# Linear attention on one core: loads and stores for 16 heads at once, with K and V on interleaved partitions

## The chip, the cores and the metric

One core of one Trainium2 chip. The metric is the device time of one execution in microseconds (us); lower is better. The profiled span is some 1.7 us shorter than that time. A run is called slow when it is over 1.5% above the fastest of the same kernel; only fast runs are compared.

## The reference

For 8 x 12 = 96 heads of 512 rows and 64 columns:

```python
Q_feat = np.maximum(0, Q) + 1
K_feat = np.maximum(0, K) + 1
KV = np.einsum('bhkd,bhkv->bhdv', K_feat, V)
K_sum = np.sum(K_feat, axis=2)
numerator = np.einsum('bhqd,bhdv->bhqv', Q_feat, KV)
denominator = np.einsum('bhqd,bhd->bhq', Q_feat, K_sum)
return (numerator / (denominator[:, :, :, None] + 1e-10)).astype(np.float32)
```

All tensors are fp32: 37.75 MB are read and 12.58 MB written.

## The kernel before

It works in 12 groups of 8 heads. A group loads K, V and Q (1 MB each, cast to bf16 on the way), makes features of K and Q on VectorE, multiplies K by V on TensorE (`keys_values`), transposes Q on TensorE with ScalarE copying the result out (`transposes`), and multiplies and normalises (`output`). Loads run three groups ahead, stores three behind. V lies in a block-diagonal tile of mostly zeros, so that four heads share a matmul.

```python
def load_v(g):
    for b in range(4):                       # four heads, 32 partitions each
        nc.gpsimd.dma_start(
            out=v_blk[g % NV][32 * b : 32 * b + 32, b],
            in_=v_dram[32 * b : 32 * b + 32, 2 * g : 2 * g + 2])

def keys_values(g):                          # 128 rows by 64 columns
    ...
    for c in range(C2):
        for n in range(2):
            nc.tensor.matmul(kva_ps[64 * n : 64 * n + 64],
                lhsT=kf[:, c, n, :], rhs=vb[:, :, n, c, :],
                start=(c == 0), stop=(c == C2 - 1))
    ...                                      # ScalarE copies it out

for g in range(NG - 1):
    if g:
        k_features(g)
        q_features(g)
        transposes(g - 1)
    if g >= 2:
        output(g - 2)
    keys_values(g)
    if g + AHEAD < NG:
        load_k(g + AHEAD); load_v(g + AHEAD); load_q(g + AHEAD)
    if g >= LAG:
        store(g - LAG)
last = NG - 1
k_features(last)
transposes(last - 1)
output(last - 2)
q_features(last)
keys_values(last)
transposes(last)
output(last - 1)
output(last)
for g in range(last - LAG, NG):
    store(g)                                 # the last two on SyncE, in halves
```

In these traces VectorE takes its instructions in program order: one that waits for data (8.36 us for Q at one place below) holds up everything behind it.

## Time and profile before

| | kernel before |
|---|---|
| time, median of the first runs | 127.61 us (127.33 to 127.71) |
| profiled span | 126.0 us |
| DMA rate over the span | 400 GB/s of HBM traffic |
| busiest compute engine | TensorE, 55% |

Here is what the end looks like: busy time of each engine in stretches of 4 us (from the start of the span; x is the number of instructions), then the granted TensorE clock, the mean busy share of the 16 DMA engines, and GB/s.

```profile
112.00:116.00 4.00, 2.46 (x40) 1.68 (x40) 3.83 (x11) 1.34 (x2) 0.00 (x0) 0.75 1.03 418
116.00:120.00 4.00, 0.95 (x14) 0.47 (x10) 2.05 (x5) 0.00 (x0) 0.00 (x0) 0.50 1.02 411
120.00:124.00 4.00, 0.00 (x0) 0.00 (x0) 0.00 (x0) 0.00 (x0) 0.00 (x0) 0.50 0.95 366
```

The columns of busy time are TensorE, its weight loads, VectorE, ScalarE and GpSimd. Computing ends in the second stretch (VectorE is busy for 2.05 us of it, then no more), while the DMA engines stay full for another 6 us. Stores are queued up, and computing hides beneath them. A DMA share over 1 means that packets of one engine overlap a little.

### The profile page before, as it was taken

How to read it: one execution, taken by the hardware profiler on the slowest of the kernel's cores; microseconds unless marked ns; L12 is line 12 of the kernel's file. 1: busy time of each engine (PE TensorE's matmuls, PEld its weight loads, DVE VectorE, ACT ScalarE, POOL GpSimd, SP SyncE). 2: the span in 40 equal slices, each digit the busy share in tenths (PEclk: the TensorE clock that was granted, in tenths of full speed). 3: DMA queues.
4: the chain of work that ended last, by engine and by line, in shares of the span. 5: the costliest groups of instructions: out<-in, count | busy, mean ns of one | idle time of the engine just before them, and what ended most of it. 6: DMA issues, size and time to landing. Idle time of an engine off the chain costs nothing.

```text
span 126.0 us, 2374 instructions
## 1 busy us (share of the span) xinstructions
PE 69.4 (55%) x960; PEld 51.1 (41%) x960; DVE 66.3 (53%) x155; ACT 47.1 (37%) x76; POOL 53.4 (42%) x91
## 2 busy tenths in 40 slices
PE   0000099719859089682971980890693496966100
PEld 0000087507647067462750660670562365744100
DVE  4898802077193582938607605723921944769400
ACT  7950007930645505554073054036019009290000
POOL 6695785616346156452372274263353341200000
PEclk9999999995999976999599589679869959996555
DMA  3999999999999999999999999999999999999993
GB/s 82 337 208 213 204 208 208 212 212 208 211 206 213 207 208 213 206 298 293 200 252 336 198 213 370 213 209 360 228 208 321 267 206 284 425 410 418 413 403 121
DMA packets 14186, 32.13 MB, mean 255 GB/s; under 512 B 1376, under 2 KB 1376, under 8 KB 14176
## 3 DMA queue, kind: packets, MB, share of 16 engines
q0 software_dynamic: 12816, 28.84, 98.8%
q1 hardware_dynamic: 1360, 3.15, 6.7%
q8 instruction: 7, 0.11, 0.3%
q14 instruction: 3, 0.02, 0.0%
HBM read 37.75 MB, written 12.58 MB: 400 GB/s over the span
## 4 chain that ended last, share of the span: by engine, by line
DMA 67%; DVE 9%; PE 8%; POOL 6%; issue 4%; POOLq 0%
DMA k_raw<-in_K_dram 25%; DMA q_raw<-in_Q_dram 17%; DMA v_blk<-in_V_dram 16%; DMA out_dram<-o_sb 9%; DVE o_sb L184 7%; PE kva_ps L141 5%; POOL v_blk L93 4%; POOL q_raw L100 2%; PE qt_ps L160 2%; DVE recip L183 1%; PE o_ps L173 1%; DVE qf L116 1%; POOL k_raw L86 1%; POOL zero L195 0%; POOLq L100 0%
## 5 line engine op out<-in xcount | busy, mean ns | idle before, releaser
L141 PE MATMUL kva_ps<-v_blk,kf 128*64 128x320 bf16 x384 | 40.6, 385 | 15.8 <-DMA v_blk<-in_V_dram 15.8
L141 PEld LDWEIGHTS <-kf 128*64 128x64 bf16 x384 | 27.9, 143 | 24.8 <-DVE qf L116 15.8
L93 POOL DMA_DIRECT2D v_blk<-in_V_dram x48 | 26.3, 552 | 27.0 <-DMA k_raw<-in_K_dram 14.8
L173 PE MATMUL o_ps<-kva_diag,qt 128*64 128x130 bf16 x384 | 19.1, 234 | 32.0 <-DVE o_sb L184 31.3
L184 DVE TENSOR_TENSOR o_sb<-o_ps,recip 128x512 f32<-128x512 f32 x48 | 33.2, 691 | 1.6
L151 ACT CAST kva_diag<-kva_ps 64x256 bf16<-64x256 f32 x24 | 8.9, 372 | 65.2 <-PE kva_ps L141 64.9
L161 ACT COPY qt<-qt_ps 128x1024 bf16<-128x1024 bf16 x24 | 29.5, 1301 | 0.3
L173 PEld LDWEIGHTS <-qt 128*64 128x64 bf16 x384 | 12.7, 114 | 37.5 <-DVE o_sb L184 35.8
L116 DVE TENSOR_SCALAR qf<-q_raw 128x1024 bf16<-128x1024 bf16 x24 | 9.2, 424 | 32.9 <-DMA q_raw<-in_Q_dram 32.9
L116 DVE TENSOR_SCALAR kf<-k_raw 128x1024 bf16<-128x1024 bf16 (+1 forms) x24 | 10.9, 497 | 10.3 <-DMA k_raw<-in_K_dram 10.3
L107 POOL DMA_DIRECT2D out_dram<-o_sb x10 | 7.7, 774 | 16.1 <-DMA q_raw<-in_Q_dram 7.8
L160 PE MATMUL qt_ps<-identity,qf 128*128 128x128 bf16 x192 | 13.1, 223 | 0.0
L160 PEld LDWEIGHTS <-qf 128*128 128x128 bf16 x192 | 11.1, 99 | 3.4 <-issue 3.2
L183 DVE RECIPROCAL recip<-o_ps 128x8 f32<-128x8 f32 x48 | 9.5, 198 | 4.1 <-PE o_ps L173 4.1
L86 POOL DMA_DIRECT2D k_raw<-in_K_dram x11 | 7.8, 713 | 8.4 <-DMA out_dram<-o_sb 3.7
L100 POOL DMA_DIRECT2D q_raw<-in_Q_dram x12 | 8.8, 730 | 4.4 <-DMA v_blk<-in_V_dram 2.5
L152 ACT CAST kva_diag<-kva_ps 64x4 bf16<-64x4 f32 x24 | 4.0, 168 | 0.0
L206 DVE MEMSET v_blk<- 128x2925 f32 x1 | 2.5, 2496 | 0.7 <-DVE ones L202 0.7
L224 DVE MEMSET v_blk<- 128x2925 f32 x1 | 2.5, 2496 | 0.6 <-issue 0.6
L212 DVE MEMSET v_blk<- 128x2925 f32 x1 | 2.5, 2496 | 0.6 <-issue 0.6
L219 POOL MEMSET kva_diag<- 128x520 bf16 x3 | 2.0, 720 | 0.0
L207 ACT COPY v_blk<-zero 128x2195 f32<-128x2195 f32 x1 | 2.0, 2020 | 0.0
(15 smaller groups left out, 7.9 us busy)
## 6 DMA issues: line engine op xcount, KB each, us to landing
out_dram<-o_sb POOLq DMA_DIRECT2D x10, 1024.0 KB, 12.1
q_raw<-in_Q_dram POOLq DMA_DIRECT2D x12, 512.0 KB, 11.1
v_blk<-in_V_dram POOLq DMA_DIRECT2D x48, 128.0 KB, 9.5
k_raw<-in_K_dram POOLq DMA_DIRECT2D x11, 512.0 KB, 12.0
out_dram<-o_sb SPq DMA_DIRECT2D x4, 512.0 KB, 7.6
k_raw<-in_K_dram SPq DMA_DIRECT2D x1, 1024.0 KB, 5.0
```

The lines of the kernel that those rows point to most:

```text
L86: (nc.sync if g == 0 else nc.gpsimd).dma_start(out=k_raw, in_=k_dram[:, g * 2 : g * 2 + 2])
L93: nc.gpsimd.dma_start(out=v_blk[g % NV][32 * b : 32 * b + 32, b], in_=v_dram[32 * b : 32 * b + 32, 2 * g : 2 * g + 2],)
L100: nc.gpsimd.dma_start(out=q_raw, in_=q_dram[:, g * 2 : g * 2 + 2])
L107: nc.gpsimd.dma_start(out=o_to, in_=o_sb)
L116: nc.vector.tensor_scalar(out=dst, in0=src, scalar1=1.0, scalar2=1.0, op0=ALU.add, op1=ALU.max)
L141: nc.tensor.matmul(kva_ps[64 * n : 64 * n + 64], lhsT=kf[:, c, n, :], rhs=vb[:, :, n, c, :], start=(c == 0), stop=(c == C2 - 1),)
L151: nc.scalar.copy(out=kva[ps, :, n, 0:D], in_=kva_ps[ps, 0:4, :])
L160: nc.tensor.transpose(qt_ps[:, c, :], qf[:, half * C + c, :, :], identity)
L161: nc.scalar.copy(out=qt[:, :, :, half], in_=qt_ps)
L173: nc.tensor.matmul(ops[c // 4][64 * j : 64 * j + 64, c // 2 % 2, (c % 2) * W : (c % 2) * W + W], lhsT=qt[:, c, 32 * b : 32 * b + 32, :], r ...
L183: nc.vector.reciprocal(out=recip, in_=cells[:, :, :, :, D:D1])
L184: nc.vector.tensor_tensor(out=o_sb[:, h:NP:2, 4 * i : 4 * i + 4].rearrange("p n (b c) d -> p b c n d", b=2), in0=cells[:, :, :, :, 0:D], i ...
```

## The change

The intent is fewer and larger transfers. The unit of loads and stores becomes a stage of 16 heads (2 MB a tensor, six stages), each still computed as two groups. K and V come in two DMAs, each to every second partition, so that a partition half holds one head of each of two pairs. V's block tile then needs two blocks instead of four, and the first matmul becomes two row tiles of 64 rows by 128 columns. The loop and its end are rewritten for stages. The diff, cut to its core:

```diff
-    def load_v(g):
-        for b in range(4):
+    def load_v(s):
+        for e in range(2):
             nc.gpsimd.dma_start(
-                out=v_blk[g % NV][32 * b : 32 * b + 32, b],
-                in_=v_dram[32 * b : 32 * b + 32, 2 * g : 2 * g + 2],
+                out=v_blk[s % IN_BUFS][e:P:2, M * e : M * e + M],
+                in_=v_dram[e, :, M * s : M * s + M],
             )
...
         for c in range(C2):
-            for n in range(2):
+            for r in range(2):
+                ps = slice(64 * r, 64 * r + 64)
                 nc.tensor.matmul(
-                    kva_ps[64 * n : 64 * n + 64],
-                    lhsT=kf[:, c, n, :],
-                    rhs=vb[:, :, n, c, :],
+                    kva_ps[:, r, 0 : NB * D],
+                    lhsT=kf[ps, c, :, :],
+                    rhs=vb[ps, :, c, :],
...
+        for g in range(2, NG - 2):
+            k_features(g)
+            q_features(g)
+            if g > 2:
                 transposes(g - 1)
+            output(g - 2) if g > 2 else None
+            keys_values(g)
+            if g % 2:
+                s = g // 2
+                store(s - 1)
+                if s + 2 < NS:
+                    load_k(s + 2)
+                    load_v(s + 2)
+                    load_q(s + 2, parts=2 if s + 2 == NS - 1 else 1)
+        a, b = NG - 2, NG - 1
+        k_features(a)
+        k_features(b)
+        transposes(a - 1)
+        output(a - 2)
+        keys_values(a)
+        output(a - 1)
+        keys_values(b)
+        store(NS - 2)
+        q_features(a)
+        transposes(a)
+        q_features(b)
+        transposes(b)
+        output(a)
+        output(b)
+        store(NS - 1)                        # four pieces on SyncE
```

More of the change, by code (lines that the diff above doesn't have):

```diff
@@ L13 @@
 BANK = 512
-IN_BUFS = 4
-OUT_BUFS = 6
-LAG = 3
-AHEAD = 3
+IN_BUFS = 3
+OUT_BUFS = 3
 @with_exitstack
@@ L42 @@
     C2 = 2 * C
-    NPAIR = B * H * S // (P * C)
-    NP = 4
-    NG = NPAIR // NP
+    M = 4
+    NS = B * H // (4 * M)
+    NG = 2 * NS
     D1 = D + 1
     W = 2 * D1
-    def view(t, c):
-        return t.flatten_outer_dims().rearrange("(n p c) d -> p n c d", p=P, c=c)
-    q_dram = view(Q, C2)
-    k_dram = view(K, C2)
-    v_dram = view(V, C2)
-    o_dram = view(out, C)
+    NB = 5
+    q_dram = Q.flatten_outer_dims().rearrange("(m p c) d -> p m c d", p=P, c=C2)
+    k_dram, v_dram = (
+        t.flatten_outer_dims().rearrange("(m e q c) d -> e q m c d", e=2, q=64, c=C2)
+        for t in (K, V)
+    )
+    o_dram = out.flatten_outer_dims().rearrange("(n p c) d -> p n c d", p=P, c=C)
     const = ctx.enter_context(tc.tile_pool(name="const", bufs=1))
@@ L63 @@
     recip_pool = ctx.enter_context(tc.tile_pool(name="recip", bufs=4))
-    psum_kva = ctx.enter_context(tc.tile_pool(name="psum_kva", bufs=2, space=bass.MemoryType.PSUM))
+    psum_kva = ctx.enter_context(tc.tile_pool(name="psum_kva", bufs=1, space=bass.MemoryType.PSUM))
     psum = ctx.enter_context(tc.tile_pool(name="psum", bufs=2, space=bass.MemoryType.PSUM))
@@ L68 @@
     identity = const.tile([P, P], BF16, name="identity")
-    NV = 3
-    v_blk = [const.tile([P, 5, 2, C2, D], BF16, name=f"v_blk{i}") for i in range(NV)]
-    ones = const.tile([P, 4], BF16, name="ones")
+    v_blk = [const.tile([P, 2 * NB, C2, D], BF16, name=f"v_blk{i}") for i in range(IN_BUFS)]
+    ones = const.tile([P, 2], BF16, name="ones")
     zero = const.tile([P, 1], FP32, name="zero")
-    kva_diag = [const.tile([P, 4, 2, D1], BF16, name=f"kva_diag{i}") for i in range(NV)]
+    kva_diag = [const.tile([P, 4, 2, D1], BF16, name=f"kva_diag{i}") for i in range(3)]
     k_in = {}
@@ L80, with load_k @@
     outs = {}
-    def load_k(g):
-        k_raw = (head_pool if g == 0 else in_pool).tile(
-            [P, 2, C2, D], FP32 if g == 0 else BF16, name="k_raw"
-        )
-        (nc.sync if g == 0 else nc.gpsimd).dma_start(
-            out=k_raw, in_=k_dram[:, g * 2 : g * 2 + 2]
-        )
-        k_in[g] = k_raw
-    def load_v(g):
-        for b in range(4):
+    def load_k(s):
+        k_raw = in_pool.tile([P, M, C2, D], BF16, name="k_raw")
+        for e in range(2):
+            nc.gpsimd.dma_start(out=k_raw[e:P:2], in_=k_dram[e, :, M * s : M * s + M])
+        for g in range(2):
+            k_in[2 * s + g] = k_raw[:, g:M:2]
@@ L93, in load_v @@
+    def load_v(s):
+        for e in range(2):
             nc.gpsimd.dma_start(
-                out=v_blk[g % NV][32 * b : 32 * b + 32, b],
-                in_=v_dram[32 * b : 32 * b + 32, 2 * g : 2 * g + 2],
-            )
-    def load_q(g):
-        q_raw = in_pool.tile([P, 2, C2, D], BF16, name="q_raw")
-        nc.gpsimd.dma_start(out=q_raw, in_=q_dram[:, g * 2 : g * 2 + 2])
-        q_in[g] = q_raw
-    def store(g):
-        o_sb = outs.pop(g)
-        o_to = o_dram[:, g * NP : g * NP + NP]
-        if g < NG - 2:
-            nc.gpsimd.dma_start(out=o_to, in_=o_sb)
-            return
-        for h in range(2):
-            nc.sync.dma_start(out=o_to[:, h:NP:2], in_=o_sb[:, h:NP:2])
@@ L112, in edge, with load_q @@
-    def edge(i):
-        return v_blk[i][:, 4, :, :, 0:4].rearrange("p n c j -> p (n c) j")
+                out=v_blk[s % IN_BUFS][e:P:2, M * e : M * e + M],
+                in_=v_dram[e, :, M * s : M * s + M],
+            )
+    def load_q(s, parts=1):
+        q_raw = in_pool.tile([P, M, C2, D], BF16, name="q_raw")
+        for i in range(parts):
+            nc.gpsimd.dma_start(
+                out=q_raw[:, i:M:parts], in_=q_dram[:, M * s + i : M * s + M : parts]
+            )
+        for g in range(2):
+            q_in[2 * s + g] = q_raw[:, g:M:2]
@@ new lines, in load_first_q, with store @@
+    def load_first_q():
+        for g in range(2):
+            q_raw = head_pool.tile([P, 2, C2, D], BF16 if g else FP32, name=f"q_first{g}")
+            (nc.gpsimd if g else nc.sync).dma_start(out=q_raw, in_=q_dram[:, g:M:2])
+            q_in[g] = q_raw
+            if g == 0:
+                load_k(0)
+    def store(s):
+        o_sb = outs.pop(s)
+        o_to = o_dram[:, 2 * M * s : 2 * M * (s + 1)]
+        if s < NS - 2:
+            nc.gpsimd.dma_start(out=o_to, in_=o_sb)
+        elif s < NS - 1:
+            nc.sync.dma_start(out=o_to, in_=o_sb)
+        else:
+            for i in range(4):
+                nc.sync.dma_start(out=o_to[:, i : 2 * M : 4], in_=o_sb[:, i : 2 * M : 4])
@@ L136, in keys_values @@
         kf = kfs.pop(g)
-        vb = v_blk[g % NV]
-        kva_ps = psum_kva.tile([P, 5, D], FP32, name="kva_ps")
+        vb = v_blk[g // 2 % IN_BUFS][:, g % 2 : 2 * NB : 2]
+        kva_ps = psum_kva.tile([P, 2, BANK], FP32, name="kva_ps")
         for c in range(C2):
-            for n in range(2):
+            for r in range(2):
+                ps = slice(64 * r, 64 * r + 64)
                 nc.tensor.matmul(
-                    kva_ps[64 * n : 64 * n + 64],
-                    lhsT=kf[:, c, n, :],
-                    rhs=vb[:, :, n, c, :],
+                    kva_ps[:, r, 0 : NB * D],
+                    lhsT=kf[ps, c, :, :],
+                    rhs=vb[ps, :, c, :],
                     start=(c == 0),
@@ L147, in keys_values @@
                 )
-        kva = kva_diag[g % NV]
+        kva = kva_diag[g % 3].rearrange("p (e r) n x -> p r e n x", r=2)
         for n in range(2):
             ps = slice(64 * n, 64 * n + 64)
-            nc.scalar.copy(out=kva[ps, :, n, 0:D], in_=kva_ps[ps, 0:4, :])
-            nc.scalar.copy(out=kva[ps, :, n, D], in_=kva_ps[ps, 4, 0:4])
+            nc.scalar.copy(
+                out=kva[ps, :, :, n, 0:D],
+                in_=kva_ps[ps, :, 0 : 4 * D].rearrange("p r (e n x) -> p r e n x", e=2, n=2)[
+                    :, :, :, n, :
+                ],
+            )
+            nc.scalar.copy(out=kva[ps, :, :, n, D], in_=kva_ps[ps, :, 4 * D : 4 * D + 2])
     def transposes(g):
@@ L164, in output @@
     def output(g):
-        kva = kva_diag[g % NV]
+        kva = kva_diag[g % 3]
         qt = qts.pop(g)
-        o_sb = out_pool.tile([P, NP, C, D], FP32, name="o_sb")
+        if g % 2 == 0:
+            outs[g // 2] = out_pool.tile([P, 2 * M, C, D], FP32, name="o_sb")
+        o_sb = outs[g // 2]
         for h in range(2):
@@ L184, in output @@
                 nc.vector.tensor_tensor(
-                    out=o_sb[:, h:NP:2, 4 * i : 4 * i + 4].rearrange(
+                    out=o_sb[:, 2 * (g % 2) + h : 2 * M : 4, 4 * i : 4 * i + 4].rearrange(
                         "p n (b c) d -> p b c n d", b=2
@@ L191, in output, with prepare_v, ones_v @@
                 )
-        outs[g] = o_sb
+    def prepare_v(i):
+        flat = v_blk[i].rearrange("p b c d -> p (b c d)").bitcast(FP32)
+        width = flat.shape[1]
+        part = width * 4 // 7
+        nc.vector.memset(flat[:, 0:part], 0.0)
+        nc.scalar.copy(out=flat[:, part:width], in_=zero.to_broadcast([P, width - part]))
+    def ones_v(i):
+        nc.vector.tensor_copy(
+            out=v_blk[i][:, 2 * M : 2 * NB, :, 0:2].rearrange("p g c e -> p (g c) e"),
+            in_=ones[:, None, :].to_broadcast([P, 2 * C2, 2]),
+        )
@@ L194 @@
     with tc.manual_schedule():
         nc.gpsimd.memset(zero, 0.0)
-        load_k(0)
-        load_q(0)
-        load_k(1)
-        load_q(1)
-        nc.vector.memset(ones, 0.0)
-        for b in range(4):
-            nc.vector.memset(ones[32 * b : 32 * b + 32, b : b + 1], 1.0)
-        flat = [t.rearrange("p b n c d -> p (b n c d)").bitcast(FP32) for t in v_blk]
-        width = flat[0].shape[1]
-        part = width * 4 // 7
-        nc.vector.memset(flat[0][:, 0:part], 0.0)
-        nc.scalar.copy(
-            out=flat[0][:, part:width], in_=zero.to_broadcast([P, width - part])
-        )
@@ L210 @@
-        nc.vector.tensor_copy(out=edge(0), in_=ones[:, None, :].to_broadcast([P, 2 * C2, 4]))
-        load_v(0)
-        nc.vector.memset(flat[1][:, 0:part], 0.0)
-        nc.scalar.copy(
-            out=flat[1][:, part:width], in_=zero.to_broadcast([P, width - part])
-        )
-        nc.vector.tensor_copy(out=edge(1), in_=ones[:, None, :].to_broadcast([P, 2 * C2, 4]))
-        make_identity(nc, identity)
+        load_first_q()
+        prepare_v(0)
+        make_identity(nc, identity)
+        load_v(0)
@@ L218 @@
         for t in kva_diag:
             nc.gpsimd.memset(t, 0.0)
+        prepare_v(1)
+        with nc.allow_low_precision("a single one in each sum"):
+            nc.vector.reduce_sum(
+                out=ones,
+                in_=identity.rearrange("p (k e) -> p e k", e=2),
+                axis=mybir.AxisListType.X,
+            )
+        ones_v(0)
+        q_features(0)
+        k_features(0)
+        transposes(0)
+        q_features(1)
+        ones_v(1)
+        load_k(1)
         load_v(1)
+        load_q(1)
@@ L221 @@
+        prepare_v(2)
+        ones_v(2)
         load_k(2)
-        k_features(0)
-        q_features(0)
-        nc.vector.memset(flat[2][:, 0:part], 0.0)
-        nc.scalar.copy(
-            out=flat[2][:, part:width], in_=zero.to_broadcast([P, width - part])
-        )
-        nc.vector.tensor_copy(out=edge(2), in_=ones[:, None, :].to_broadcast([P, 2 * C2, 4]))
         load_v(2)
         load_q(2)
-        for g in range(NG - 1):
-            if g:
-                k_features(g)
-                q_features(g)
+        keys_values(0)
@@ L235 @@
+        k_features(1)
+        transposes(1)
+        output(0)
+        keys_values(1)
+        for g in range(2, NG - 2):
+            k_features(g)
+            q_features(g)
+            if g > 2:
                 transposes(g - 1)
-            if g >= 2:
-                output(g - 2)
+            output(g - 2) if g > 2 else None
             keys_values(g)
-            if g + AHEAD < NG:
-                load_k(g + AHEAD)
-                load_v(g + AHEAD)
-                load_q(g + AHEAD)
@@ L243 @@
-            if g >= LAG:
-                store(g - LAG)
-        last = NG - 1
-        k_features(last)
-        transposes(last - 1)
-        output(last - 2)
-        q_features(last)
-        keys_values(last)
-        transposes(last)
-        output(last - 1)
-        output(last)
-        for g in range(last - LAG, NG):
-            store(g)
+            if g % 2:
[5 more added lines that the diff above has]
+                    load_q(s + 2, parts=2 if s + 2 == NS - 1 else 1)
```

## The prediction

> **What bounds the kernel now.** I read the page's slices first. The DMA row is the only one that is full from end to end; no compute engine is busy for more than 55% of the span.
>
> ```profile
> PE   0000099719859089682971980890693496966100
> DVE  4898802077193582938607605723921944769400
> DMA  3999999999999999999999999999999999999993
> GB/s 82 337 208 213 204 208 208 212 212 208 211 206 213 207 208 213 206 298 293 200 252 336 198 213 370 213 209 360 228 208 321 267 206 284 425 410 418 413 403 121
> HBM read 37.75 MB, written 12.58 MB: 400 GB/s over the span
> ```
>
> The GB/s row counts bytes as they are written. Loads are cast from fp32 to bf16, so 208 GB/s written is 416 GB/s read; the last six slices (from 107 us) are stores alone at 403 to 425. So the engines run at one rate whatever they carry, and the 126.0 us span is 50.33 MB of HBM traffic plus a start and an end. The chain that ended last says the same, and then names the end:
>
> ```profile
> DMA 67%; DVE 9%; PE 8%; POOL 6%; issue 4%; POOLq 0%
> ```
>
> The waits show what compute waits for (columns: engine and line, releaser, us in total, times, longest):
>
> ```profile
> DVE qf L116 <- DMA q_raw<-in_Q_dram: 32.9, 9, 4.5
> POOL v_blk L93 <- DMA k_raw<-in_K_dram: 14.8, 9, 2.4
> ```
>
> VectorE waits for Q. GpSimd waits for an earlier DMA before it issues the next: the built order shows each GpSimd DMA waiting for the eighth one before it. Neither starves the queues, as the DMA row stays at 9.
>
> Third, I counted the trace's DMA packet records: 8,960 cast loads (4 KB read, 2 KB written), 2,560 packets of 4 KB of GpSimd stores, 1,024 of 2 KB of SyncE stores, 256 of SyncE's 4 KB loads, and 1,376 completion packets (16 per DMA). A fit of these counts over 4 us windows from 6 to 106 us (to 122 us for SyncE's) gives the engine time of each: 155.3 ns a cast load, 155.6 ns a 4 KB store packet, 79.1 ns a 2 KB one, about 19.5 ns a completion packet. I take 155.3 for SyncE's loads too. Over 16 engines: 87.0 + 24.9 + 5.1 + 2.5 + 1.6 = 121.0 us, which with about 5 us of start and end is the span. Mixing loads and stores changes nothing in the fit.
>
> **What the Trainium skill says.** "DMA: Bandwidth & Descriptors", section "Where 436 GB/s comes from", puts the fabric's ceiling at 435 GB/s; the 416 to 425 here agree, so little is left to win in rate. Its section "Anatomy of one DMA" gives about 2 us of fixed cost per DMA and advises large ones; here up to eight are in flight and that cost is hidden, the engine time of a completion being the 19.5 ns above. "TensorEngine Tiling (Array Packing)", sections "Available Configurations" and "Restrictions", lists 64x128 as two row tiles that run in parallel, and says column tiling (the form before) disables fast weight load. No run yet shows the new form; the old one overlapped: 32 matmuls took 2.34 us, 73 ns each. "TensorE: Matmul & The Clock Gate", section "What's actually happening", says idleness for some 3.4 us halves the clock. The trace agrees: PEclk falls to 5 tenths in slices after idle ones, and the same 32 matmuls then take 4.01 us.
>
> **The change, part by part.**
>
> 1. *DMAs.* From the built order: 35 on GpSimd (was 81) and 6 on SyncE (was 5). Loads keep their 4 KB rows, so 8,960 cast packets stay: 87.0 us. Four 2 MB stores go by GpSimd (2,048 packets, 19.9 us), the last two groups by SyncE (2,048 of 2 KB, 10.1 us), the first Q by SyncE 2.5 us, completions 35 x 16 x 19.5 / 16 ns = 0.7 us. Sum 120.2 against 121.0: **0.8 us gained**, nearly all of it 46 completions.
>
> 2. *First matmul.* Still 16 x 2 matmuls of 320 columns for a group, now 64 rows by 128 columns. I keep 2.34 us warm and 4.01 us cold. Half of the products are thrown away, at no cost. Its PSUM tile is single, but ScalarE's copies (about 1 us) end before the next group's matmuls start.
>
> 3. *Start.* SyncE still brings 1 MB first, now of Q; GpSimd's first load follows. I see no change in when the queues fill. Fewer small VectorE fills; nothing there is on the path.
>
> 4. *Middle.* A store of stage s-1 (16 heads) now waits until Q of stage s has landed and its outputs are made. From the walk below that takes 12 us after Q lands. The queue then still holds a store and a stage of loads, 5.0 + 15.1 = 20 us. It doesn't run dry; 8 us to spare.
>
> 5. *End.* Here is the cost. Before, the last load ended at 106.9 us with seven 1 MB stores behind it (7.3 MB, 18 us), and compute ended at 118 us, beneath them. After, three 2 MB stores (6.3 MB, 15.1 us) follow the last load, but two groups are still to be computed out of it. The durations come from the timeline of the kernel before, which starts at a Q landing as the new end does:
>
> ```profile
> 97.28 0.76 DVE L116 TENSOR_SCALAR qf<-q_raw 128x1024 bf16<-128x1024 bf16 x2 [4.49 <-DMA q_raw<-in_Q_dram]
> ...
> 100.03 4.01 PE L141 MATMUL kva_ps<-v_blk,kf 128*64 128x320 bf16 x32
> ...
> 103.98 1.07 PE L160 MATMUL qt_ps<-identity,qf 128*128 128x128 bf16 x16
> ...
> 107.51 2.34 PE L141 MATMUL kva_ps<-v_blk,kf 128*64 128x320 bf16 x32
> ...
> 110.88 2.46 ACT L161 COPY qt<-qt_ps 128x1024 bf16<-128x1024 bf16 x2
> ```
>
> Let T be when the last load lands. In engine time the loads (89.5), three stores (14.9) and 34 completions (0.7) are 105.1 us before it. The same sum for the kernel before is 103.4 and its last load ended at 106.9, an offset of 3.5. So T = 108.6. Q of stage 4 (groups 8, 9) lands a store and three loads earlier, at T - 20.1, and is seen 0.4 us later. From there VectorE and TensorE hand work to each other without a wait for data. In us after that moment:
> - features, then output(6): to 4.1; keys_values(8) cold 2.8 to 6.8; transposes(8) to 7.8; output(7) 8.2 to 11.6 (store 3 may go); keys_values(9) warm 10.2 to 12.6; transposes(9) to 13.6. All as at 97.28 to 110.85.
> - output(8) 14.0 to 17.4; keys_values(10) warm 16.0 to 18.4 (its V landed at about 15.1); output(9) 18.8 to 22.1: store 4 may go, at T + 2.4, while store 3 still moves. Good.
> - keys_values(11) 20.9 to 23.2; transposes(10) to 24.2; ScalarE's copies of keys_values (1.0) and of the transposes (2.5) to 26.8; transposes(11) end after the second of those, 27.3. The program has output(10) behind transposes(11): 27.7 to 31.1; output(11) to 34.6.
>
> So the last piece is issued at T - 19.7 + 34.6 = T + 14.9. A SyncE load took 1.1 us from issue to first packet; the piece's 0.5 MB take 1.3 us; the span ended 1.3 us after the last packet. End: T + 18.6 = **127.2 us**, where stores without a gap would give T + 15.1 + 1.3 = 125.0. The exposed tail is 2.2 us; the sum is -0.8 + 2.2, about +1.2 after roundings of the offset. Time was 1.7 us over the span, so 128.9. I add 0.3 for a chance that keys_values(10) or (11) falls into a cold clock (1.7 us each): **129.2 us**.
>
> **The rivals.**
> - *The end is hidden after all.* For: the four-piece last store lets data go early, and the author's order has all keys_values first. Against: ScalarE's copies stand before output(10). It would make 125.2 + 1.7 = 126.9 us.
> - *Large transfers raise the rate.* For: the skill's advice. Against: the fit leaves only completions to save. A 2% higher rate would make about 125 to 127.
> - *Row tiles don't overlap, or stay cold.* For: nothing in this trace tests them, and weights are twice as wide. Against: the page. Unpaired matmuls would add 2 us or more in each of four keys_values of the end: 133 to 137 us.
> - *The queues run dry in the middle*, as stores wait longer at the head of GpSimd's order. Against: 8 us to spare. Each gap of 1 us costs 1 us, unless under the tail.
>
> **Range and chances.** The walk has some 14 links, each good to a few tenths, and the clock adds up to 3 us; being hidden takes 2.3 off. So 126.6 to 131.6 holds it 8 times in 10. Faster by over 2% needs under 125.1 us, below what the DMA sum allows: 4%. Slower by over 2% is over 130.2: 22%. The rest, 74%, is within 2%.
>
> **What will show it.** Step 1: 656 completion packets, DMA full until about 118 us, loads at 208 to 212 GB/s. Step 2: 32 matmuls in about 2.3 or 4.0 us. Step 4: no slice under 9 in the DMA row from 2 to 110 us. Step 5: the last load lands near 108.6; VectorE works until about 123.5 us, 15 us after it (before: 11); DMA gaps between the four last pieces; the chain's end is VectorE and TensorE work rather than queued stores. Wrong would be a DMA row full to the last slice (the end hidden), holes in the middle (starved), or keys_values well over 4 us (tiles not parallel).

## The result

| | before | after |
|---|---|---|
| time, median | 127.66 us (127.33 to 127.76, 4 runs) | 131.23 us (130.39 to 132.33, 4 runs) |
| profiled span | 126.0 us | 128.9 us |
| last store landed (the trace's completion records) | 125.06 us | 127.61 us |
| completion packets | 1,376 | 656 |

The ratio is 1.029 (95% interval 1.020 to 1.038): slower. Ratios here are the mean time of one kernel's fast runs over the mean of the other's of the same rounds, so not quite the ratio of the medians quoted. The time lies in the predicted range, but 2.0 us above the point, and on the side that had been given 22%.

The page after, the slices first:

```profile
PE   0040029786459101978600896900496968755630
DVE  5862650290395007929004928300965875923970
PEclk9999999999999855599996589997569999999555
DMA  4999999999999999999999999999999999999474
GB/s 90 323 205 208 212 201 210 212 209 213 210 212 215 208 248 409 281 205 210 212 217 386 354 201 209 211 215 337 390 227 208 212 210 285 411 362 369 194 311 163
HBM read 37.75 MB, written 12.58 MB: 390 GB/s over the span
```

The DMA row is full until the last three slices (about 119 us on) and then drops to 4, 7 and 4. VectorE, which had been idle in the last slices, is at 9 and 7 beside it. Middle and rate are nearly unchanged: 201 to 215 GB/s in the first twelve slices of loads alone (204 to 213 before). The chain that ended last, by engine, has turned from transfers toward computing:

```profile
DMA 52%; DVE 20%; PE 18%; POOL 3%; issue 2%; ACT 2%
```

The groups and the longest waits (formats as in the prediction):

```profile
L149 PE MATMUL kva_ps<-v_blk,kf 64*128 64x320 bf16 x384 | 33.9, 336 | 9.7 <-DMA v_blk<-in_V_dram 8.6
...
POOL out_dram L115 <- DVE o_sb L199: 64.0, 4, 16.8
...
DVE qf L123 <- DMA q_raw<-in_Q_dram: 30.7, 4, 8.8
```

The new first matmul is not slower (33.9 us busy against 40.6 before; 8 of the 12 groups ran at the full clock, 4 of 12 before). GpSimd waits 16 us for each store's outputs, which is harmless while the queue is long. VectorE has four waits for Q, one a stage, up to 8.8 us each. The last one starts the end. Its timeline:

```profile
90.06 0.76 DVE L123 TENSOR_SCALAR qf<-q_raw 128x1024 bf16<-128x1024 bf16 x2 [8.36 <-DMA q_raw<-in_Q_dram]
...
93.14 3.56 PE L149 MATMUL kva_ps<-v_blk,kf 64*128 64x320 bf16 x32
...
100.26 2.35 PE L149 MATMUL kva_ps<-v_blk,kf 64*128 64x320 bf16 x32
...
106.17 2.35 PE L149 MATMUL kva_ps<-v_blk,kf 64*128 64x320 bf16 x32
...
111.09 2.35 PE L149 MATMUL kva_ps<-v_blk,kf 64*128 64x320 bf16 x32
...
112.38 0.38 SPq L117 DMA_DIRECT2D out_dram<-o_sb  x1
...
119.76 5.48 SPq L120 DMA_DIRECT2D out_dram<-o_sb  x4
...
124.15 0.69 DVE L199 TENSOR_TENSOR o_sb<-o_ps,recip 128x512 f32<-128x512 f32 x1
```

From the moment VectorE sees Q of stage 4 (90.06) to its last instruction (124.84) there are 34.8 us in which VectorE, TensorE and ScalarE hand work to each other. SyncE issues the last store's four pieces between 119.76 and 125.2, as they come out. In stretches, with the columns of before:

```profile
112.00:116.00 4.00, 2.63 (x42) 1.94 (x39) 1.70 (x5) 2.42 (x6) 0.00 (x0) 1.00 0.94 361
116.00:120.00 4.00, 2.22 (x44) 1.67 (x43) 1.93 (x6) 3.25 (x3) 0.00 (x0) 0.94 0.81 313
120.00:124.00 4.00, 3.01 (x40) 1.83 (x36) 3.86 (x10) 0.00 (x0) 0.00 (x0) 0.50 0.67 263
```

Where the kernel before had VectorE idle and the DMA engines full, this one has VectorE at 3.86 of 4 us and the DMA engines at two thirds.

### The profile page after: what moved, and what is told of

The parts are those of the page before. It is cut to its first block, busy times and chain, and to the rows that moved or that the text cites. A ratio compares the mean times of both kernels' runs of the same rounds, so it can differ in the third digit from the quotient of the medians.

```text
span 128.9 us, 2293 instructions
## 1 busy us (share of the span) xinstructions
PE 66.5 (52%) x960; PEld 46.3 (36%) x960; DVE 64.6 (50%) x151; ACT 47.0 (36%) x76; POOL 26.5 (21%) x45
## 4 chain that ended last, share of the span: by engine, by line
DMA 52%; DVE 20%; PE 18%; POOL 3%; issue 2%; ACT 2%
DMA q_raw<-in_Q_dram 39%; DMA k_raw<-in_K_dram 12%; DVE o_sb L199 12%; PE kva_ps L149 11%; DVE v_blk L212 4%; PE qt_ps L173 4%; PE o_ps L188 3%; DVE recip L198 3%; ACT qt L174 2%; POOL k_raw L83 2%; DVE qf L123 1%; POOL v_blk L89 1%; POOL out_dram L115 1%; DVE ones L231 0%
## 5 line engine op out<-in xcount | busy, mean ns | idle before, releaser
L188 PE MATMUL o_ps<-kva_diag,qt 128*64 128x130 bf16 x384 | 20.4, 245 | 35.8 <-DVE o_sb L199 35.4
L149 PE MATMUL kva_ps<-v_blk,kf 64*128 64x320 bf16 x384 | 33.9, 336 | 9.7 <-DMA v_blk<-in_V_dram 8.6
L149 PEld LDWEIGHTS <-kf 64*128 64x128 bf16 x384 | 20.7, 106 | 20.4 <-DVE kf L123 9.3
L123 DVE TENSOR_SCALAR qf<-q_raw 128x1024 bf16<-128x1024 bf16 x20 | 7.5, 419 | 30.7 <-DMA q_raw<-in_Q_dram 30.7
L198 DVE RECIPROCAL recip<-o_ps 128x8 f32<-128x8 f32 x48 | 9.5, 198 | 20.9 <-PE o_ps L188 20.9
L115 POOL DMA_DIRECT2D out_dram<-o_sb x4 | 3.6, 911 | 64.0 <-DVE o_sb L199 64.0
L123 DVE TENSOR_SCALAR kf<-k_raw 128x1024 bf16<-128x1024 bf16 x24 | 9.0, 418 | 2.8 <-DMA k_raw<-in_K_dram 2.3
L89 POOL DMA_DIRECT2D v_blk<-in_V_dram x12 | 7.5, 635 | 4.7 <-DMA v_blk<-in_V_dram 2.2
L213 ACT COPY v_blk<-zero 128x2195 f32<-128x2195 f32 x3 | 6.0, 2021 | 0.0
L97 POOL DMA_DIRECT2D q_raw<-in_Q_dram x6 | 4.6, 782 | 3.1 <-DMA k_raw<-in_K_dram 3.1
L123 DVE TENSOR_SCALAR qf<-q_first 128x1024 bf16<-128x1024 f32 (+1 forms) x4 | 2.1, 564 | 1.7 <-DMA q_first<-in_Q_dram 1.7
```

Source lines behind the costliest of these rows:

```text
L89: nc.gpsimd.dma_start(out=v_blk[s % IN_BUFS][e:P:2, M * e : M * e + M], in_=v_dram[e, :, M * s : M * s + M],)
L123: nc.vector.tensor_scalar(out=dst, in0=src, scalar1=1.0, scalar2=1.0, op0=ALU.add, op1=ALU.max)
L149: nc.tensor.matmul(kva_ps[:, r, 0 : NB * D], lhsT=kf[ps, c, :, :], rhs=vb[ps, :, c, :], start=(c == 0), stop=(c == C2 - 1),)
L188: nc.tensor.matmul(ops[c // 4][64 * j : 64 * j + 64, c // 2 % 2, (c % 2) * W : (c % 2) * W + W], lhsT=qt[:, c, 32 * b : 32 * b + 32, :], r ...
L198: nc.vector.reciprocal(out=recip, in_=cells[:, :, :, :, D:D1])
L213: nc.scalar.copy(out=flat[:, part:width], in_=zero.to_broadcast([P, width - part]))
```

## The experiments

The theory: the end chain from stage 4's Q is exposed. The main rival: the larger transfers are themselves slower. A third question was whether the new form of loads and matmul costs anything. Twelve runs were made, on four chips. Every run but the three that say so gave the correct result.

**Only the end's order.** The last stage's first Q work is moved ahead of `output(9)`:

```diff
         keys_values(a)
+        q_features(a)
+        transposes(a)
         output(a - 1)
         keys_values(b)
         store(NS - 2)
-        q_features(a)
-        transposes(a)
         q_features(b)
```

> Changed kernel, but in the end alone: the features and transposes of group 10's Q go ahead of output(9) and keys_values(11), so that ScalarE copies them while it is idle. Theory (the end chain of VectorE and TensorE from the landing of stage 4's Q is exposed, and sets the end): output(10) starts right after the transposes of group 11, VectorE ends near 122.7 us of the span instead of 124.8, and the span shrinks by about 2 us, 127 us; time 128.5 to 129.5. Rival (the larger transfers themselves, or their uneven landing on the 16 DMA engines, cost the time): nothing in the transfers is changed, so the time stays at 131 within 0.7. Correct result.

Measured: 129.68 us (129.40 to 130.11), ratio 1.011 to the kernel before (1.004 to 1.017); last landing 127.07. The changed kernel: its ratio was 1.029 and, later, 1.026. It was run at another time. No transfer changed, so the rival's "stays at 131" falls. The gain is smaller than forecast (128.5 to 129.5). This timeline line of TensorE says why:

```profile
93.27 4.45 PE L149 MATMUL kva_ps<-v_blk,kf 64*128 64x320 bf16 x32
```

`keys_values(8)` took 4.45 us at the halved clock, against 3.56 in the changed kernel. VectorE ended 33.5 us after seeing Q (90.19 to 123.70), 1.3 less than 34.8. By this estimate the reorder saved about 2.2 and the clock took 0.9 back.

**The Q wait moved away, first try.** In the loop, `output`, `keys_values` and `transposes` now come in this order before `q_features`:

```diff
             k_features(g)
-            q_features(g)
-            if g > 2:
-                transposes(g - 1)
             output(g - 2) if g > 2 else None
             keys_values(g)
+            if g > 2:
+                transposes(g - 1)
+            q_features(g)
```

(The end is reordered too: both outputs of stage 4 before the key-value matmuls of stage 5.)

> Changed kernel, but the features of Q of a group come after the outputs and the key-value matmuls of the groups before, in the loop and in the end, and both outputs of stage 4 come before the key-value matmuls of stage 5. No work waits any more for a Q that it does not need. Theory (exposed end chain): outputs 6 to 9 are made before the last loads have landed, the chain of the end starts only at the last landing (near 110 us), VectorE ends near 120.5 us, the stores run without a gap and the span is 126 to 127 us, time 127.5 to 128.7, near the kernel before; the spread of the runs falls to that of before (under 0.5 us). Rival (transfers are slower): the last load lands at 110 as before and the DMA is then full, but the time stays near 131. Correct result.

Measured: 140.65 us (140.50 to 142.07), ratio 1.098. A miss, and of my making. The chain of this kernel (start, us, what) shows a loop:

```profile
48.29 3.85 PE kva_ps L149 x32
52.15 1.01 PE qt_ps L173 x16
53.18 2.46 ACT qt L174 x2
55.68 0.44 PE o_ps L188 x8
...
58.38 3.93 PE kva_ps L149 x32
```

With the transposes behind `keys_values`, ScalarE's copies of 2.46 us no longer lie beside those matmuls but on the path, and one group takes 10.1 us (48.29 to 58.38), all of the 10 us that its transfers take. From 37 us on, `keys_values` takes 3.7 to 4.0 us in every group, with the clock halved for part of it. This kernel is no test of the theory. It shows what the original order was hiding.

**The new form, but 8 heads at once.** Interleaved halves, two-head V blocks and row tiles, with the sizes, order, buffers and end of the kernel before:

```diff
-    M = 4
+    M = 2                                   # 8 heads: a stage is one group
     NS = B * H // (4 * M)
-    NG = 2 * NS
+    NG = NS
...                                          # loop and stores as in the kernel before
```

> The changed kernel's form (K and V by two halves of interleaved partitions, V blocks for two heads, first matmul 64 rows by 128 columns), but 8 heads at once, with the order, the buffers and the ends of the kernel before; 67 DMAs on GpSimd. Theory (the exposed end of two groups out of one stage is the cost, the form is neutral): 127.0 to 128.2, the same as before, perhaps 0.3 less by fewer completions (14 of GpSimd's DMAs less at about 0.02 us each). Rival (row tiles, or loads to interleaved partitions of 64, cost the time): 130 to 131, with landings as spread as in the changed kernel (2.7 us from the first to the last engine near the end against 1.8 before). Correct result.

Measured: 127.95 us (127.94 to 127.99) against 128.10 for the kernel before, ratio 0.997 (0.990 to 1.004): the same. Its DMA row is full to the end:

```profile
DMA  2999999999999999999999999999999999999992
```

The completions of its last load spread over 1.8 us, as in the kernel before. So neither the row tiles, nor the loads to every second partition, nor the V blocks cost any time here, where computing lies beneath the transfers. What costs comes with 16 heads at once.

**All loads in halves, the stages kept.** Each K, V and Q load is issued as two of half the size, one for each group.

> Changed kernel with its order kept, but every load of K, V and Q in two of half the size, as large as those of the kernel before or smaller; 16 heads still at once. Theory (exposed end chain): 30 more DMAs cost some 0.6 us of engine time, and fewer bytes in flight may make landings 0.5 us less uneven: 130.5 to 132, no gain. Rival (large single transfers, and how unevenly 16 engines finish them, are what costs): near 128 to 129, spread of landings back to 1.8 us. Correct result.

Measured: 128.33 and 129.94 us in two fast runs, 130.64 and 131.06 in two slow ones; ratio 1.006 (0.994 to 1.018), unclear. My expectation had overlooked that half a Q load is all that the first group needs. The profile shows VectorE seeing Q at 87.34 instead of 90.06. Both theories could claim this run, so two more took it apart.

**Q in halves alone, and K and V in halves alone**, with the changed kernel run again on the same chip.

```diff
-    def load_q(s, parts=1):
+    def load_q(s, parts=2):                 # Q in halves; the other kernel
                                             # splits K and V the same way
```

> The changed kernel itself, once more, so that the others of this call have it on the same chip, and for a second profile of it. Theory (the end chain of VectorE and TensorE is exposed): 130.4 to 132.3 as before; VectorE ends 34.8 us after the Q of stage 4 has been seen, or 36.5 where one more of the four key-value groups of the end runs at the halved clock. Rival (the transfers vary): the chain's length is the same in both profiles and the landing of Q of stage 4 moves instead.

Measured: 131.03 us (130.52 to 131.25), ratio 1.026 (1.022 to 1.029). VectorE saw Q at 90.53 and ended at 125.33, 34.8 us later, exactly as in the first profile. That is the sign that had been given to the rival: what made this span 0.5 us longer was the landing of Q, not the clock.

> Changed kernel, but every Q load in two of 1 MB, one for each group, as its last stage already has it; K and V as large as in the changed kernel. Theory (the end chain starts when the first group of stage 4 has its Q): that half lands 2.5 us earlier, so the chain starts 2.5 us earlier, until it meets the landing of the last V: the time falls by 1.5 to 2.5 us, to 128.5 to 129.5. Rival (fewer bytes in flight and more even landings made the split of all loads faster): no gain from this one, 130.5 to 131.5. Correct result.

Measured: 129.77 and 129.80 us in the fast runs (132.1 and 132.3 in the slow ones), ratio 1.016 (1.012 to 1.021), 1.2 us below the changed kernel on the same chip. That gain rests on two runs of four: the median of all four is 130.94, and one of the slow ones was granted no lower a clock (0.834 and 0.856 in the slow, 0.854 in the fast). What the trace shows is firmer. The end in this kernel's profile, VectorE's line and then TensorE's:

```profile
87.31 0.76 DVE L123 TENSOR_SCALAR qf<-q_raw 128x1024 bf16<-128x1024 bf16 x2 [6.56 <-DMA q_raw<-in_Q_dram]
```

```profile
105.27 2.35 PE L149 MATMUL kva_ps<-v_blk,kf 64*128 64x320 bf16 x32 [1.25 <-DMA v_blk<-in_V_dram]
```

The chain started 2.8 us earlier, as the theory says, and then ran into the landing of the last V (the bracket: 1.25 us idle, released by the V load). A new wait, and `keys_values(8)` at 4.07 us instead of 3.56, took most of the gain; VectorE ended at 123.87, 1.0 us earlier than in the first profile.

> Changed kernel, but every load of K and V in two of half the size, Q of 2 MB left whole. Theory (exposed end chain from Q's landing): no gain; 24 more DMAs cost about 0.5 us of engine time: 130.5 to 132. Rival (fewer bytes in flight and more even landings made the split of all loads faster): 128.5 to 129.5, with the spread of landings near the end at 1.8 to 2 us instead of 2.5 to 2.7. Correct result.

Measured: 131.33 us (130.00 to 131.79), ratio 1.025 (1.019 to 1.031): no gain, and the last load's completions still spread over 2.7 us from the first DMA engine to the last (2.0 in the changed kernel of this call). So smaller K and V loads do not help; that form of the rival is refuted. This profile also shows the clock. VectorE saw Q at 90.07, as in the changed kernel, yet ended 36.3 us later instead of 34.8:

```profile
PEclk9999999999955996589975569995559999996555
```

Beside the row of the changed kernel, the slices near 90 us are all at half speed (555 where it has 756: halved from 87.1 to 97.4 us instead of 88.8 to 95.7), and the end falls off 1.7 us earlier. `keys_values(8)` took 4.40 us instead of 3.56.

**The Q wait moved away, second try.** Q's work comes last in a stage, but the transposes stay ahead of the matmuls that hide them:

```diff
+        for s in range(1, NS - 1):
+            g = 2 * s
+            k_features(g)
+            if s > 1:
+                transposes(g - 1)
+                output(g - 2)
+            keys_values(g)
+            k_features(g + 1)
+            output(g - 1)
+            keys_values(g + 1)
+            store(s - 1)
+            ...                             # loads of stage s + 2
+            q_features(g)
+            transposes(g)
+            q_features(g + 1)
```

(The end follows the same idea.)

> Changed kernel; the features and transposes of a stage's Q come at the end of that stage's work, after the outputs of the stage before and both key-value groups; the transposes stay ahead of the key-value matmuls that hide ScalarE's copies, unlike in the first try, whose loop took 10.3 us a group. Theory (exposed end chain that starts at the landing of stage 4's Q): nothing waits for a Q that it doesn't need, outputs 8 and 9 are made by about 104 us, VectorE ends near 120.5 us, 10 us after the last landing, the four last pieces find the queue still full or nearly so, span 126 to 127, time 127.7 to 128.7. Rival (the transfers of the changed kernel are slower): time stays above 130 with the DMA row full. Correct result.

Measured: 128.73 us (128.52 to 128.95), ratio 1.008 (1.005 to 1.011); 2.3 us below the changed kernel on the same chip. VectorE ended at 122.46, 2.0 us later than forecast, and the last store landed at 125.68:

```profile
DMA  4999999999999999999999999999999999999983
```

With unchanged transfers and the same arithmetic, order alone recovers 2.3 of the 3.3 us. The last 1.0 us stays. The 2.0 us by which VectorE was late are the size of one `keys_values` of the end, which fell into the halved clock (4.34 us instead of 2.35):

```profile
106.58 4.34 PE L149 MATMUL kva_ps<-v_blk,kf 64*128 64x320 bf16 x32 [1.71 <-DVE kf L123]
```

**The transfers by themselves.** Both kernels with the computing taken out. The results are wrong: stores send a constant, and the last stores wait for the last Q.

> Wrong result on purpose: the kernel before with its computing taken out. The same DMAs in the same order through the same queues and buffers; the stores send a constant, and the last two groups' stores on SyncE wait for the last Q, as the computing would make them. The sum of packet counts says that transfers alone set the time of the kernel before: 121.0 us of engine time and about 5 us of start and end: span 125.5 to 126.3, the same as with computing.

> Wrong result on purpose: the changed kernel with its computing taken out, its DMAs as they are, the last two stages' stores on SyncE waiting for the last Q. Theory (exposed computing in the end is what costs; by the packet counts the transfers are 0.8 us shorter): span 124.8 to 125.5, below the one without computing of the kernel before. Rival (the larger transfers are themselves less well served, as the mean landing of stage 4's Q 0.8 us later than the packet sum suggests): span 126 to 127, about 0.5 us or more above that of the kernel before.

Measured: the DMA rows are, first of the kernel before and then of the changed one, both without computing:

```profile
DMA  3999999999999999999999999999999999999940
```

```profile
DMA  3999999999999999999999999999999999999991
```

The times (129.69 and 127.88 us) can't be compared directly. The first kernel's span, 128.3 us, missed its forecast of 125.5 to 126.3, and not by its transfers: the program ended 3.2 us after its last store had landed (0.9 in the second), and the wait is not one for data:

```profile
SPq L245 <- PEq L245: 3.0, 2, 2.5
```

SyncE's queue waited for TensorE's queue in the closing barrier; why it is so long there stays open. The completions of the last store are what tells:

| last store landed, us | with computing | without |
|---|---|---|
| before | 125.06 | 125.09 |
| after | 127.61 | 125.37 |

Each figure is from one profile, and the runs of one kernel here differ by 0.4 us and more. So the kernel before is bound by its transfers, to well within that noise. The changed kernel's transfers alone landed 0.28 us later than before: too little to call a loss, but the gain of 0.8 that the packet count promised isn't there. Its span of 126.2 us lies where the rival had put it (126 to 127), not the theory (124.8 to 125.5). Its computing adds 2.24 us (2.74 by the second profile of the changed kernel), where the prediction said 2.2. So both are at work: mostly exposed computing, and transfers some 1 us worse than their sum.

**Smaller stores, without computing.** Each of GpSimd's four 2 MB stores as two of 1 MB.

> Wrong result on purpose: the changed kernel without computing, and each of GpSimd's four stores of 2 MB in two of 1 MB, as large as those of the kernel before; loads unchanged. With computing out, the changed kernel's last store landed at 125.4 us where the packet counts say 124.3, and most of the loss came between 30 and 60 us, around the first 2 MB store. Theory A (the large stores cause it): the 16 engines' packets between 30 and 60 us come to 30.0 us of engine time instead of 29.5, the spread of landings stays below 1 us, last landing near 124.6, time 127.0 to 127.4. Theory B (the loads to every second partition in 1 MB pieces, or the amount in flight, cause it): no change, last landing 125.2 to 125.6, time 127.6 to 128.2.

Measured: 127.81 us (127.28 to 128.40), within theory B's range; last landing 125.01, between the two forecasts. Engine time delivered (the packets that ended in a stretch, each times its engine time from the prediction, over 16 engines) was 29.57 us from 30 to 60 us (29.46 without the split, 30.07 in the kernel before); completions of the last load spread over 1.4 us instead of 2.4. It makes landings more even, but it does not bring the lost engine time back: where that goes stays open. No 16-head run had small loads and small stores at once, or less data in flight.

**A version that should have matched the kernel before.** The second try, with the last stage's loads by group (K, V and Q of group 10, then those of group 11).

> Correct result. The reordered version with Q's work at the end of a stage, and in the last stage alone the loads come by group: K, V and Q of group 10 first, then those of group 11, so that the first group is computed while the second still loads. Theory (what is left of the end is exposed computing): VectorE ends about 9 us after the last landing, the four last pieces wait for the queue and not for VectorE, span 125.6 to 126.6, time 127.3 to 128.3, at or slightly below the kernel before. Rival (the transfers of 16-head stages are slower): not below 128.3, with the DMA row full to the end.

Measured: one fast run of 128.28 us, five slow ones of 131.30 to 132.97; no ratio, and a miss. The profile fell in a slow run. Three of its end's four `keys_values` took 4.4 us, at half clock, with TensorE idle for 1.6 to 1.8 us at or just before each, and VectorE ended at 127.5. But its last load also landed late, at 111.42 us, its completions spread over 3.3 us. With no profile of the fast run, what moves this kernel by 3 to 4.7 us isn't shown. No version tried beats the kernel before; the 8-head one ties with it.

## Why the prediction was right or wrong

- **What bounds the kernel: right.** Without computing, the last store lands at the same time (125.09 against 125.06 us).
- **First matmul: right.** 32 matmuls took 2.35 us at the full clock (2.34 forecast). At the halved one they took up to 4.45, not 4.01: in the prediction's "cold" example the clock was halved for 3.4 of the 4.0 us only (100.4 to 103.8).
- **Its pointers to the skill: two are a section off.** That row tiles run in parallel stands in "Key Properties" of the tiling page, and the advice of large DMAs in "Rules for kernel authors" of the DMA page.
- **Start and middle: right.** No hole in the DMA row before the end. The store of stage 3 was issued at 101.83, 11.8 us after Q; the forecast was "12 us after Q lands".
- **The end chain: right.** 34.8 us against 34.6 from Q's arrival to VectorE's last instruction, with `keys_values` at 93.1, 100.3, 106.2 and 111.1, that is 3.1, 10.2, 16.1 and 21.0 us in (forecast 2.8, 10.2, 16.0, 20.9). Computing out, the exposed part is 2.24 us (2.2); so close a match is partly luck, as a second profile gives 2.74. Moving its order moves the time; halving the K and V loads alone does not. The last load landed at 110.33 us, not near 108.6, and VectorE ended 14.5 us after it (15 forecast).
- **The DMA sum: wrong, and this is the step that failed.** "Sum 120.2 against 121.0: **0.8 us gained**" measured as no gain (0.28 us later, within noise). The completions saved were counted; the loss between 6 and 60 us was not (23.95 + 29.46 us of engine time delivered without computing, against 24.17 + 30.07 for the kernel before: 0.8 us), nor that a landing waits for the slowest of 16 DMA engines. The loss is no accident of one profile: recounted in all of them, this sum is 54.1 to 54.2 us in the three 8-head kernels and 52.4 to 53.8 in all eleven profiles with 16 heads. Without computing, the last load's completions spread over 2.4 us (1.8 in the kernel before), Q of stage 4 over 2.2. So Q of stage 4 was seen at 90.06, not at 88.9 (T - 19.7 of the forecast), and the whole chain moved by 1.2 us. How these 1.2 us divide between lost engine time and uneven landings isn't measured. The rival "large transfers raise the rate" is refuted as well; the engine time delivered has the opposite sign, and its cause is open.
- **The finish:** the span ended 1.3 us after the last landing (0.9 before) and 4.1 us after VectorE; the forecast had 3.7.
- **The clock allowance: too small.** The profiled run took 130.71 us; the four runs have a median of 131.23 and a spread of 1.9 us, where those before have 0.4. That contrast didn't repeat: later the runs of each spread by 0.7 us. That the halved clock lengthens the chain is shown in the profile of the kernel with K and V in halves. That it makes the differences between runs is not shown: the two profiles of the changed kernel differ by the landing of Q instead.

Together: 127.2 forecast for the span, plus 1.2 (Q later), 0.2 (chain) and 0.35 (finish) gives the 128.9 measured. The rest up to 2.0 us is the runs, less the 0.3 that was allowed for them.

## What to carry to other kernels

When transfers bound a kernel, count first what fewer and larger DMAs can save: here only completions, 0.8 us by the sum, and even that didn't show. Look at what the last unit of work leaves uncovered instead. Walk the chain from the last wait that it depends on, often a landing one unit earlier than the last. An end chain that is exposed also takes on the state of the TensorE clock: one `keys_values` took 3.56 us in one profile and 4.40 in another.

## What the Trainium skill lacked or had wrong

- "DMA: Bandwidth & Descriptors", section "Rules for kernel authors", says to use DMAs of at least 1 MiB and to coalesce. Here 41 DMAs instead of 86, the stores of 2 MB, gave no gain: last landing without computing 125.37 us against 125.09. The rule doesn't say that it stops paying once many DMAs are in flight: the fixed cost of about 2 us (section "Anatomy of one DMA") was hidden with up to eight DMAs in flight, and a completion took about 20 ns of an engine.
- The same page, section "Why a DMA increments its semaphore by 16 and not by 1", says that a DMA's semaphore counts 16 engines that finish independently. It has no figure for how far they drift apart in a long stream: here 0.2 to 0.7 us from first to last at the start, and near the end 1.8 (8 heads) or 1.9 to 3.3 (16 heads, with computing).
- "TensorEngine Tiling (Array Packing)", section "Restrictions", says that column tiling disables fast weight load. Row tiles freed of that were no faster: 2.35 us against 2.34 for 32 matmuls of 320 columns, though a weight load took 106 ns in the mean instead of 143. That weight loads lie beside the matmuls in both would explain it; no run tests that.
- "TensorE: Matmul & The Clock Gate" has the halved clock after idleness, with which the runs agree (2.35 and 4.45 us for the same matmuls). Its section "What's actually happening" says that the phase of the clock's window varies from run to run, and puts the ramp at under 1% of a typical span. Where the end chain was exposed and had gaps, one kernel took 128.3 to 133.0 us, over 3%; how much of this the clock makes is not shown.
